# Quarter-sized modulation loads, softmax division before the transposes, and a PSUM tile each for gate and up

## Chip, cores and metric

One core of a Trainium2 chip runs the whole program. The metric is device microseconds of one execution, as the median of the runs shown. TensorE does the matrix products, VectorE, ScalarE and GpSimd the elementwise work, SyncE (SP) issues nearly all transfers. PSUM is the accumulator memory of TensorE's products, in banks of 128 partitions x 512 fp32 numbers; SBUF is the on-chip working memory.

## The reference

Two layers work on 256 latent tokens `x` and 256 context tokens `ctx`, of 1024 numbers each. All data are fp32. Each layer:

```
sh1, sc1, g1, sh2, sc2, g2 = split(silu(c) @ w_mod + b_mod)     # the same for ctx with c_ctx
h   = rms_norm(x) * (1 + sc1) + sh1
a_q, a_k, a_v, conv_u, c_q, c_k, c_v = split(h @ w_in)
mix = [global attention (6 heads), convolution of 31 taps, window attention (6 heads, with a sink)]
x   = x + g1 * (mix @ w_out)
h   = rms_norm(x) * (1 + sc2) + sh2
y   = per token, 2 of 32 experts:  (silu(h @ w_gate[e]) * (h @ w_up[e])) @ w_down[e]
x   = x + g2 * weighted sum of y
```

`w_mod` is 1024 x 6144 a layer, so one modulation vector (shift, scale or gate) needs a 1024 x 1024 block of it, 4 MiB. An expert has three matrices of 1024 x 512, 2 MiB each. Attention's keys are 512 tokens (latent and context); the softmax is exp(score - max) divided by its sum over the keys. The second layer updates only the latent tokens, and the output is their RMS norm.

## The kernel before

**Layer 0's start.** SP issues loads in the order of lines 493 to 499. For j = 0 and 2 it loads four of the eight 128-column chunks of the scale vector (m = 1, in transfers of 512 KB through `load_k4`) and of the shift vector (m = 0, in transfers of 1 MiB), 2 MiB each; for every j the rows 256j to 256j + 255 of `w_in`'s key and value columns (`load_kv`, 512 KB) and of the first convolution columns (`load_u`, 512 KB). `mod_load` (lines 263 to 313) makes a function for each such part. Its `products` multiply `silu(c)` as a 32-column stationary operand in four strips of 32 partitions; its `compute` copies the sums to SBUF on ScalarE (`ms`, line 288), may run other work in between (`between`), picks the rows out and turns them with tiny matmuls (line 295), and adds the bias on VectorE (line 302), with two more VectorE operations for a scale vector (lines 309, 310).

`modulate` (lines 346 to 380) gives three steps for a 128-row chunk k of the hidden state: `h_mul` (VectorE, needs the scale), `h_scale` (ScalarE, needs the shift; writes the rounded high part) and `h_shift` (VectorE, the rest). The products of k want those two parts and the two parts of each weight: `split_w` (lines 382 to 388) for key and value columns on ScalarE and VectorE, `split_u` (523 to 530) for convolution columns on ScalarE and GpSimd. Each product is three matmuls (high by high, high by low, low by high): `product_kv(k)` has twelve, into four PSUM banks `pk`, and `product_u(k)` six, into the tile `pu`. The order of ScalarE, TensorE and VectorE is written out by hand in lines 568 to 609: modulations 0 and 1, dummy matmuls, then eight k, with modulations 2 and 3 around `product_u` of k = 1 and 2. Outside such blocks a planner with a timeline simulation orders the instructions.

**Attention units.** `unit(g, j, i)` (lines 808 to 874) is for a pair of heads and one block of 128 query tokens (i < 2, all 512 keys) or both context blocks (i = 2, 256 keys). It makes scores `S`, takes the max (VectorE, line 825), P = exp on ScalarE with sums collected beside it (line 839), the sums' reciprocal `rl`, transposes P on TensorE (line 853), copies it to `PT` and multiplies by V into `po`. Then `rl` is spread over 64 partitions by a matmul with the identity into the other half of `po` (line 866), copied by ScalarE (`ars`, 870) and multiplied in by VectorE (871), and the result is split into a high part (`mh`, 873) and a low part (874). Layer 0 has 18 units, 12 of one block and 6 of two; layer 1 has 12 of one block. In layer 0 other work, such as the taps of the convolution on VectorE, stands beside them.

**The MoE.** Two experts at a time make a pair, 16 pairs a layer, ordered by hand on TensorE, VectorE and ScalarE (line 1596). `pair` (lines 1344 to 1414) has one stationary tile per expert with up to 64 tokens. It loads twelve tiles of 1 MiB (gate, up and down, two halves for each of two experts) through a ring of 8 slots. Gate (m = 0) goes into half 0 of a two-bank PSUM tile `pgu` and up (m = 1) into half 1, 32 matmuls each; `sil` = silu of half 0 is ScalarE's (line 1358), issued between the two. `act` = up x weight x `sil` is VectorE's (line 1363). Then come four transposes, the down products into the two-bank tile `py`, and `split_y` (lines 1267 to 1276), which reads `py` into YH (ScalarE) and YL (VectorE). `P2` hands out two-bank tiles from a ring of 2, so `pgu` and `py` alternate.

Four lists `at` (lines 1607 to 1622), emptied by `burst(0)` to `burst(3)`, put other work between these steps: the gather of later pairs' tokens, and `adders`, which add the pair before's result to the residual. In most of layer 0's pairs `burst(0)`, which stands between gate and up, has at most VectorE's `onehot`; in layer 1 it has up to three adders, with products of TensorE.

Of the kernel before, what the change touches and what calls it, by code (L numbers as in the profile page):

```python
# [10 lines left out]
F32 = mybir.dt.float32  # L11
# [25 lines left out]
def trunk(ctx: ExitStack, tc: tile.TileContext, t_in, rope, out, cfg):  # L37
# [426 lines left out]
    def layer(l):  # L464
# [27 lines left out]

        first = []
        for j in range(4):
            if l == 0 and j % 2 == 0:
                first += [mod_load(0, 1, 2 * j, 4, load_k4), mod_load(0, 0, 2 * j, 4)]
            load_kv(j)
            if l == 0:
                load_u(j)
# [53 lines left out]
        def mul_to(k):  # L553
            while muls and muls[0] <= k:
                h_mul(muls.pop(0))
# [4 lines left out]
        def product_kv(k, wh, wl, tiles=range(4)):  # L560
            for i in tiles:
                for n, (ww, hh) in enumerate(passes(k, wh, wl)):
                    pe.matmul(pk[i], hh(k, 128 * i, 128), ww, start=k == 0 and n == 0, stop=k == KC - 1 and n == 2)
            if l > 0 and k in cf[0]:
                fill(True)

        order = ExitStack()
        if l == 0:

            order.enter_context(tc.manual_schedule(engines={ET.Activation, ET.PE}))  # L570
            pm = P2("pm")
            pu = P2("pu")
            sk, su = {}, {}

            def modulation(i, work=None):
                first[i](eng=ve, between=work, p=(pm[:, 0, 128 * i:128 * i + 128], pm[:, 1, 16 * i:16 * i + 16]))

            def parts(k):
                h_scale(k)
                h_shift(k)  # L580

            def splits(k):
                sk[k] = split_w(wKV(k), 512, "w", eng=ve)
                su[k] = split_u(k, 0)

            def dummies(n):

                for _ in range(n):
                    pe.matmul(pm[:, 1, 256:512], identb, masks.rearrange("p a b -> p (a b)"), start=True, stop=True)

            modulation(0)
            mul_to(3)
            dummies(4)
            modulation(1)
            dummies(12)
            splits(0)
            parts(0)
            for k in range(KC):
                if k + 1 < KC:
                    splits(k + 1)  # L600
                    parts(k + 1)
                product_kv(k, *sk[k])
                if k in (1, 2):
                    modulation(k + 1, lambda: product_u(pu, k, su[k]))
                    mul_to(k + 3)
                else:
                    product_u(pu, k, su[k])
                    if k > 2:
                        mul_to(k + 3)
        else:  # L610
            for k in range(KC):
                if k + 1 < KC:
                    mul_to(k + 1)
                    h_scale(k + 1)
                h_shift(k)
                product_kv(k, *ws.next())
# [191 lines left out]
        def unit(g, j, i):  # L808
# [37 lines left out]
                ve.tensor_tensor(lsum, lsum, es, op=OP.add)  # L846
            rl = sm.tile([128, 4], F32, name="rl")[:, :n]
            ve.reciprocal(rl, lsum)
            PT = K4("PT", (128, 2, 512))
            for h in range(2):  # L850
                pt = P1("pT")
# [4 lines left out]
            for b in range(nb):  # L856
                for kt in range(4 // nb):
                    for h in range(2):
# [2 lines left out]
                                  V[:, kt if i < 2 else 2 + kt, cv_:cv_ + 64],  # L861
                                  PT[:, h, 128 * (b * 2 + kt):128 * (b * 2 + kt) + 128],
                                  start=kt == 0, stop=kt == 4 // nb - 1)
            for b in range(nb):
                for h in range(2):
                    pe.matmul(po[64 * h:64 * h + 64, 256 + 128 * b:384 + 128 * b],
                              rl[:, h * nb + b:h * nb + b + 1].to_broadcast([128, 64]), ident, start=True, stop=True)
            nq = 128 * nb
            rs = K2("ars", (128, nq), tag="a")
            sc.copy(rs, po[:, 256:256 + nq])  # L870
            ve.tensor_tensor(rs, po[:, 0:nq], rs, op=OP.mult)
            mh = qT[g](2 * j, 128 * i, nq)
            sc.copy(mh, rs)
            ve.tensor_tensor(qT[g](2 * j + 1, 128 * i, nq), rs, mh.bitcast(F32), op=OP.subtract)

        conv(len(taps))
        n = 0
# [466 lines left out]
        def pair(pr, xg, ws, burst, final, finish):  # L1344


            p = P2("pgu")
            for m in range(2):
                for a in range(2):
                    w_ = (load_rows_two([weights_of(pr, m, a, e) for e in range(2)], "we") if final else  # L1350
                          [weight(m, a, e, pr) for e in range(2)])
                    for k in range(4 * a, 4 * a + 4):
                        for e in range(2):
                            pe.matmul(p[64 * e:64 * e + 64, m, :], xg[:, k, 64 * e:64 * e + 64], w_[e](k % 4),  # L1354
                                      start=k == 0, stop=k == KC - 1)
                if m == 0:
                    sil = K2("sil", tag="w")
                    sc.activation(sil, p[:, 0], AF.Silu)  # L1358
                    if final:
                        sqrt_table(sil)  # L1360
                    burst(0)
            act = K2("act", tag="w")
            ve.scalar_tensor_tensor(act, p[:, 1], ws, sil, op0=OP.mult, op1=OP.mult)  # L1363
            burst(1)
            pt = P1("pat")
            for f in range(4):
# [325 lines left out]
```

## Time and profile before

| what | value |
|---|---|
| median of 3 runs (lowest, highest) | 1475.16 us (1473.77, 1477.0) |
| the profiled execution's own time | 1472.71 us |
| span of the profiled execution | 1470.7 us |
| mean granted clock of TensorE | 0.986 of full |
| TensorE busy | 1390.8 us, 95% of the span |
| VectorE busy | 613.4 us, 42% |
| ScalarE busy | 395.7 us, 27% |
| GpSimd busy | 76.7 us, 5% |
| transfers | 481.86 MB, mean 328 GB/s |

The profiled execution's own time is 2.01 us above its span, for what lies around it. Times within the trace are microseconds from the span's start. By the labels of the instructions, the first products of layer 0 run to about 66 us, attention of layer 0 lies between 145 and 235, its MoE between 300 and 815, attention of layer 1 between 873 and 950, and its MoE from 1000 to the end. The busy share is an average over these; TensorE counts as busy while a matmul is in its pipeline, so a share of 100% says that it did not pause, not that it worked at its peak. The DMA share is the mean busy share of the core's 16 DMA engines. In brackets behind an instruction stands how long its engine was idle before it, and what ended this.

### The profile page before, as it was taken

Reading aid. Unit: us, or ns where it says so; the run is one execution under the profiler, and the core shown is the slowest. Engines: PE = TensorE matmul, PEld = TensorE weight load, DVE = VectorE, ACT = ScalarE, POOL = GpSimd, SP = SyncE. Lnnn points to the kernel's source line nnn. Section 1 sums busy time; section 2 is a strip of 40 time slices with the busy share of each in tenths; the row PEclk is TensorE's granted clock in tenths of the full one; section 3 lists DMA queues with packets and bytes.
Section 4 is the critical chain, followed back from the end, with each engine's and each line's share of the span. In section 5 each row is a group of like instructions: output and inputs, shape, how many; then the busy total and the mean of one; then the engine's idle time right before and its main releaser. Section 6 shows DMA issues by size and latency. Waiting matters only on the chain. (4 is left out here: it accounts for less than half of the span.)

```text
span 1470.7 us, 20485 instructions
## 1 busy us (share of the span) xinstructions
PE 1390.8 (95%) x8068; PEld 771.3 (52%) x8068; DVE 613.4 (42%) x1380; ACT 395.7 (27%) x954; POOL 76.7 (5%) x132
## 2 busy tenths in 40 slices
PE   6999999999999999999998998889999999999987
PEld 5776677755445544444434776783433343333332
DVE  4379974443323423233325679853222222222223
ACT  4454675421111111101102565552111011111102
POOL 1202000100000000000001110010000000000000
PEclk9999999999999999999999999999999999999999
DMA  9757204397999999999999590186999999999996
GB/s 350 282 166 284 109 1 172 131 375 306 376 408 414 413 400 406 417 406 414 385 405 389 201 332 31 44 357 280 388 422 421 421 421 421 421 421 419 421 417 255
DMA packets 97412, 481.86 MB, mean 328 GB/s; under 512 B 14068, under 2 KB 22544, under 8 KB 52128
## 3 DMA queue, kind: packets, MB, share of 16 engines
q1 hardware_dynamic: 96576, 478.79, 81.1%
q8 instruction: 66, 1.08, 0.3%
q10 hardware_dynamic: 464, 1.11, 0.2%
q0 software_dynamic: 272, 0.59, 0.1%
q14 instruction: 34, 0.28, 0.0%
HBM read 479.42 MB, written 1.05 MB: 327 GB/s over the span
## 5 line engine op out<-in xcount | busy, mean ns | idle before, releaser
L1354 PE MATMUL pgu<-we,xg 128*64 128x512 f32 x1904 | 449.3, 598 | 30.7 <-DMA we<-in_w_gate_dram 13.6
L1354 PEld LDWEIGHTS pgu<-we,xg 128*64 128x64 f32 x1904 | 142.3, 137 | 324.1 <-issue 246.8
L1408 PE MATMUL py<-we,actT 128*64 128x512 f32 x888 | 202.9, 596 | 0.7 <-ACT actT L1369 0.7
L1363 DVE SCALAR_TENSOR_TENSOR act<-pgu,ws,sil 128x512 f32<-128x512 f32 x32 | 24.0, 751 | 285.1 <-PE pgu L1354 248.6
L1250 DVE SCALAR_TENSOR_TENSOR xT<-pc,mod,xT 128x256 f32<-128x256 f32 x256 | 104.8, 477 | 52.9 <-PE pc L1247 52.2
L1408 PEld LDWEIGHTS py<-we,actT 128*64 128x64 f32 x888 | 63.1, 137 | 117.5 <-issue 113.4
L1304 ACT COPY xg<-pg 128x256 f32<-128x256 f32 x112 | 36.3, 376 | 308.2 <-PE pg L1300 308.2
L1258 DVE TENSOR_TENSOR xo<-xo,pc 128x512 f32<-128x512 f32 x62 | 39.8, 684 | 112.0 <-PE pc L1257 112.0
L1299 PE MATMUL pg<-OH,hH 128*128 128x256 f32 x336 | 83.3, 286 | 0.0
L1300 PE MATMUL pg<-OH,hL 128*128 128x256 f32 x336 | 82.1, 283 | 0.0
L643 DVE SCALAR_TENSOR_TENSOR ca<-gpad,cw,ca 128x512 f32<-128x512 f32 (+1 forms) x120 | 74.2, 619 | 0.9
L1299 PEld LDWEIGHTS pg<-OH,hH 128*128 128x128 f32 x336 | 63.9, 190 | 7.2 <-issue 5.7
L1300 PEld LDWEIGHTS pg<-OH,hL 128*128 128x128 f32 x336 | 64.1, 191 | 0.9
L1358 ACT ACTIVATE sil<-pgu 128x512 f32<-128x512 f32 x32 | 19.1, 598 | 167.6 <-PE pgu L1354 167.6
L281 PE MATMUL pm<-wm,scT 128*32 128x256 f32 (+1 forms) x896 | 60.7, 359 | 3.0 <-DMA wm<-in_w_mod_dram 2.8
L1273 DVE TENSOR_TENSOR Yg<-py,g2r 128x512 f32<-128x512 f32 x31 | 21.3, 688 | 100.7 <-PE py L1408 96.4
L1276 DVE TENSOR_TENSOR YL<-py,YH 128x512 fp32r<-128x512 f32 x32 | 22.1, 690 | 92.7 <-ACT YH L1275 92.7
L1275 ACT CAST YH<-Yg 128x512 fp32r<-128x512 f32 x31 | 19.1, 617 | 141.2 <-DVE Yg L1273 141.2
L1275 ACT CAST YH<-py 128x512 fp32r<-128x512 f32 x32 | 18.7, 585 | 139.0 <-PE py L1408 113.8
L1377 POOL CAST se<-ident 32x128 fp32r<-32x128 f32 x32 | 9.1, 287 | 900.1 <-PE pb L1378 900.1
L1246 PE MATMUL pc<-oht,YH 128*128 128x512 f32 x128 | 53.4, 418 | 1.2 <-ACT YH L1275 1.2
L1247 PE MATMUL pc<-oht,YL 128*128 128x512 f32 x128 | 50.6, 395 | 0.2 <-DVE YL L1276 0.2
(429 smaller groups left out, 2106.0 us busy)
## 6 DMA issues: line engine op xcount, KB each, us to landing
we<-in_w_up_dram SPq DMA_DIRECT2D x112, 1024.0 KB, 9.7
we<-in_w_down_dram SPq DMA_DIRECT2D x111, 1024.0 KB, 12.4
we<-in_w_gate_dram SPq DMA_DIRECT2D x110, 1024.0 KB, 13.5
wm<-in_w_mod_dram SPq DMA_DIRECT2D x44, 1024.0 KB, 9.4
wp<-in_w_gate_dram SPq DMA_DIRECT2D x8, 1024.0 KB, 9.5
wp<-in_w_up_dram SPq DMA_DIRECT2D x8, 1024.0 KB, 9.7
we<-in_w_gate_dram SPq DMA_DIRECT2D x16, 512.0 KB, 12.1
we<-in_w_up_dram SPq DMA_DIRECT2D x16, 512.0 KB, 10.2
```

The lines of the kernel that those rows point to most:

```text
L281: pe.matmul(p[0][32 * q:32 * q + 32], scT[:, kq, :], ws[128 * kq // nr][:, kq % (nr // 128), c:c + n], start=k == 0, stop=k == KC * nq // ...
L643: ve.scalar_tensor_tensor(a, g, wt, a, op0=OP.mult, op1=OP.add)
L1246: pe.matmul(pc, YH[:, 128 * o:128 * o + 128], oht, start=True, stop=False)
L1247: pe.matmul(pc, YL[:, 128 * o:128 * o + 128], oht, start=False, stop=True)
L1250: ve.scalar_tensor_tensor(xT[:, o, sl], pc[:, sl], mod[l][:, 5, o, s:s + 1], xT[:, o, sl], op0=OP.mult, op1=OP.add)
L1258: ve.tensor_tensor(xo[t][:, sl], xo[t][:, sl], pc, op=OP.add)
L1275: sc.copy(YH[:rows, sl], py)
L1299: pe.matmul(dst, hH[t][:, 128 * k:128 * k + 128], rhs, start=t == 0, stop=False)
L1300: pe.matmul(dst, hL[t][:, 128 * k:128 * k + 128], rhs, start=False, stop=t == NT - 1)
L1304: sc.copy(xg[e][:, k - 1:k + 1, :], v[:, :, e])
L1354: pe.matmul(p[64 * e:64 * e + 64, m, :], xg[:, k, 64 * e:64 * e + 64], w_[e](k % 4), start=k == 0, stop=k == KC - 1)
L1408: pe.matmul(py[64 * e:64 * e + 64, h], actT[:, 128 * f + 64 * e:128 * f + 64 * e + 64], wd[e](f % 2)[:, 512 * h:512 * h + 512], start=f == ...
```

## The change

In layer 0's start both vectors load in quarters (two chunks, 1 MiB), one of each before every pair of k's rows, so eight modulations are computed in place of four. Two stand ahead of the products and six inside: for even k around `product_u(k)`, for odd k around `product_kv(k)`. The order by hand is written anew, with 4 and 8 dummies in place of 4 and 12, and the splits and parts of k + 1 move accordingly.

In attention, P is multiplied by the reciprocal sums in place before it is transposed, the first head's on VectorE and the second's on ScalarE. The `rl` products, the `ars` copy and the multiply are gone, and `mh` and the low part come from `po`.

In the MoE, gate and up each take a two-bank tile of `P2` of their own, and use its first bank.

```diff
-            if l == 0 and j % 2 == 0:
-                first += [mod_load(0, 1, 2 * j, 4, load_k4), mod_load(0, 0, 2 * j, 4)]
+            if l == 0:
+                first += [mod_load(0, 1, 2 * j, 2, load_k4), mod_load(0, 0, 2 * j, 2)]
             load_kv(j)
...
             def modulation(i, work=None):
-                first[i](eng=ve, between=work, p=(pm[:, 0, 128 * i:128 * i + 128], pm[:, 1, 16 * i:16 * i + 16]))
+                q = i % 4
+                first[i](eng=ve, between=work, p=(pm[:, 0, 128 * q:128 * q + 128], pm[:, 1, 16 * i:16 * i + 16]))
...
             modulation(0)
-            mul_to(3)
+            mul_to(1)
             dummies(4)
             modulation(1)
-            dummies(12)
+            dummies(8)
+            parts(0)
             splits(0)
-            parts(0)
             for k in range(KC):
-                if k + 1 < KC:
+                if k + 1 < KC and k % 2 == 0:
                     splits(k + 1)
                     parts(k + 1)
-                product_kv(k, *sk[k])
-                if k in (1, 2):
-                    modulation(k + 1, lambda: product_u(pu, k, su[k]))
-                    mul_to(k + 3)
+                if k == KC - 1:
+                    product_kv(k, *sk[k])
+                elif k % 2 == 0:
+                    product_kv(k, *sk[k])
+                    if k + 2 < KC:
+                        modulation(k + 2, lambda: product_u(pu, k, su[k]))
+                        mul_to(k + 3)
+                        splits(k + 2)
+                        continue
                 else:
-                    product_u(pu, k, su[k])
-                    if k > 2:
-                        mul_to(k + 3)
+                    modulation(k + 2, lambda: product_kv(k, *sk[k]))
+                    parts(k + 1)
+                product_u(pu, k, su[k])
...
             ve.reciprocal(rl, lsum)
+            for h in range(2):
+                for b in range(nb):
+                    e = h * nb + b
+                    p = P[:, h, w_ * b:w_ * b + w_]
+                    if h:
+                        sc.activation(p, p, AF.Identity, scale=rl[:, e:e + 1])
+                    else:
+                        ve.tensor_scalar(p, p, rl[:, e:e + 1], None, op0=OP.mult)
             PT = K4("PT", (128, 2, 512))
...
-            for b in range(nb):
-                for h in range(2):
-                    pe.matmul(po[64 * h:64 * h + 64, 256 + 128 * b:384 + 128 * b],
-                              rl[:, h * nb + b:h * nb + b + 1].to_broadcast([128, 64]), ident, start=True, stop=True)
             nq = 128 * nb
-            rs = K2("ars", (128, nq), tag="a")
-            sc.copy(rs, po[:, 256:256 + nq])
-            ve.tensor_tensor(rs, po[:, 0:nq], rs, op=OP.mult)
             mh = qT[g](2 * j, 128 * i, nq)
-            sc.copy(mh, rs)
-            ve.tensor_tensor(qT[g](2 * j + 1, 128 * i, nq), rs, mh.bitcast(F32), op=OP.subtract)
+            sc.copy(mh, po[:, 0:nq])
+            ve.tensor_tensor(qT[g](2 * j + 1, 128 * i, nq), po[:, 0:nq], mh.bitcast(F32), op=OP.subtract)
...
-            p = P2("pgu")
             for m in range(2):
+                p = P2("pgu")[:, 0]
...
-                            pe.matmul(p[64 * e:64 * e + 64, m, :], xg[:, k, 64 * e:64 * e + 64], w_[e](k % 4),
+                            pe.matmul(p[64 * e:64 * e + 64, :], xg[:, k, 64 * e:64 * e + 64], w_[e](k % 4),
...
-                    sc.activation(sil, p[:, 0], AF.Silu)
+                    sc.activation(sil, p, AF.Silu)
...
-            ve.scalar_tensor_tensor(act, p[:, 1], ws, sil, op0=OP.mult, op1=OP.mult)
+            ve.scalar_tensor_tensor(act, p, ws, sil, op0=OP.mult, op1=OP.mult)
```

## Rows read from the trace of the kernel before

**Rows 1.** windows view, MoE stretches: us, busy by engine, clock, DMA share, GB/s
```profile
400.00:680.00 280.00, 271.17 (x1381) 130.81 (x1378) 90.58 (x198) 32.90 (x72) 2.58 (x9) 1.00 1.00 409
1120.00:1340.00 220.00, 207.42 (x933) 84.63 (x931) 49.40 (x86) 27.59 (x62) 2.30 (x8) 1.00 1.01 421
```

**Rows 2.** waits view of TensorE, 400 to 680: waiter, releaser, us, times, longest
```profile
PE pgu L1354 <- ACT sil L1358: 7.3, 9, 1.1
```

**Rows 3.** tile view of sil, whole kernel: who waited (us, times)
```profile
  PE pgu L1354: 10.5, 14
```

**Rows 4.** timeline of ScalarE: first and ninth sil between 404 and 652
```profile
404.38 0.60 ACT L1358 ACTIVATE sil<-pgu 128x512 f32<-128x512 f32 x1 [5.00 <-PE pgu L1354]
...
651.20 0.60 ACT L1358 ACTIVATE sil<-pgu 128x512 f32<-128x512 f32 x1 [5.00 <-PE pgu L1354]
```

**Rows 5.** timeline of TensorE: one pair's gate products and its up products
```profile
644.03 7.04 PE L1354 MATMUL pgu<-we,xg 128*64 128x512 f32 x32
651.85 3.65 PE L1354 MATMUL pgu<-we,xg 128*64 128x512 f32 x16 [0.78 <-ACT sil L1358]
```

**Rows 6.** timeline at a pair's start: first gate product, last reader of py
```profile
330.92 7.04 PE L1354 MATMUL pgu<-we,xg 128*64 128x512 f32 x32
...
333.55 0.68 DVE L1276 TENSOR_TENSOR YL<-py,YH 128x512 fp32r<-128x512 f32 x1
```

**Rows 7.** timeline of layer 0's start, to its first key product
```profile
18.16 1.08 PE L281 MATMUL pm<-wm,scT 128*32 128x128 f32 x32
...
22.02 1.08 PE L281 MATMUL pm<-wm,scT 128*32 128x128 f32 x32 [2.78 <-DMA wm<-in_w_mod_dram]
...
24.86 0.40 ACT L528 CAST wu<-wU 128x256 fp32r<-128x256 f32 x1 [0.74 <-DMA wU<-in_w_in_dram]
...
26.32 0.78 PE L563 MATMUL pkv<-wh,hT 128*128 128x512 f32 x1
```

**Rows 8.** timeline of TensorE: the third modulation, inside the products of k=1
```profile
34.05 0.40 PE L563 MATMUL pkv<-wl,hT 128*128 128x512 f32 x1
...
36.26 0.50 PE L535 MATMUL pu<-hT,wu 128*128 128x512 f32 x1
...
37.75 0.28 PE L295 MATMUL pm<-ident,ms 128*128 128x8 f32 x2
```

**Rows 9.** windows view, two stretches of the start (as rows 1)
```profile
12.00:16.00 4.00, 3.00 (x67) 2.40 (x69) 1.51 (x7) 2.32 (x5) 0.00 (x0) 1.00 1.05 387
20.00:24.00 4.00, 1.47 (x34) 1.13 (x35) 1.18 (x4) 0.77 (x2) 0.00 (x0) 1.00 1.08 365
```

**Rows 10.** windows view, layer 0's units, first and second half (as rows 1)
```profile
150.00:189.00 39.00, 35.47 (x332) 25.95 (x326) 35.08 (x70) 25.01 (x83) 1.49 (x2) 0.96 0.18 72
189.00:217.00 28.00, 28.00 (x281) 21.86 (x280) 22.14 (x62) 20.51 (x71) 0.00 (x0) 1.00 0.01 1
```

**Rows 11.** timeline of TensorE: po and rl products, one-block and two-block unit
```profile
200.87 0.98 PE L860 MATMUL po<-PT,V 128*64 128x128 f32 x13
...
202.10 0.66 PE L853 MATMUL pT<-ident,P 128*128 128x128 f32 x4
...
205.03 0.98 PE L860 MATMUL po<-PT,V 128*64 128x128 f32 x13
...
206.49 0.66 PE L853 MATMUL pT<-ident,P 128*128 128x128 f32 x4
```

**Rows 12.** lines view by form, VectorE: op, shapes, count | busy us, mean ns
```profile
L825 DVE TENSOR_REDUCE mx<-S 128x2 f32<-128x1024 f32 x24 | 29.3, 1221 | 3.1 <-PE S L820 1.9 <-PE S L822 0.8
...
L871 DVE TENSOR_TENSOR ars<-po,ars 128x128 f32<-128x128 f32 x24 | 6.8, 285 | 3.4 <-ACT ars L870 3.4
...
L641 DVE TENSOR_SCALAR ca<-gpad,cw,vb 128x512 f32<-128x512 f32 x2 | 1.1, 542 | 0.0
```

**Rows 13.** lines view by form, ScalarE (columns as rows 12)
```profile
L870 ACT COPY ars<-po 128x128 f32<-128x128 f32 x24 | 6.4, 267 | 23.9 <-PE po L866 23.9
...
L1592 ACT ACTIVATE fs<-xo,finr 128x512 f32<-128x512 f32 x2 | 1.3, 714 | 0.9 <-DVE finr L338 0.9
```

## The prediction

> **What bounds the kernel now.** I read the page's time slices first: two long MoE stretches carry most of the span, so a change at the start or in attention can only move a few microseconds and the pair loop of the MoE needs the closest look. The windows view separates the two loops [rows 1]. In layer 0's, 271.17 us of 280 are TensorE's, and the transfers run at 409 GB/s. In layer 1's, TensorE has idle time, and they run at 421 GB/s, which is the highest steady rate in the page. So layer 1's loop is bound by transfers, and layer 0's by TensorE: in its waits the only large releaser is ScalarE's `sil`, nine times in 280 us, 7.3 us in all, and no transfer [rows 2]. Over the whole kernel it is fourteen times, 10.5 us [rows 3]. The reader is to see that this wait ends on a tile and not on its data: up's products write the other half of the tile that `sil` reads. The first and the ninth `sil` of the stretch begin 246.82 us apart [rows 4], so a pair takes 246.82/8 = 30.85 us. A pair loads twelve tiles of 1 MiB, 12.58 MB, which at 421 GB/s take 29.89 us. That is the floor under any gain there: 0.96 us a pair.
>
> At the start the order is loads, modulation, then products: the first key product starts at 26.32 us, behind a second vector's half that waited for its weights and a cast that waited for `wU` [rows 7]. In layer 0's attention, VectorE is busy for 35.08 us of the first 39, and TensorE for all of the last 28 [rows 10]: two halves with different limits.
>
> **Part 3: a tile each for gate and up.** Gate's products take 7.04 us, and up's begin 651.85 - 644.03 = 7.82 us after gate's first [rows 5]. The last matmul's drain is no part of the pitch: with 0.59 us for one (the rounded mean of the page's costliest group), 15 pitches of (7.04 - 0.59)/15 = 0.43 make 16 x 0.43 = 6.88, and a step without the wait would follow there. So a pair loses 7.82 - 6.88 = 0.94 us, less in those where other work fills part of it. A pair could win 0.94, and the floor allows 0.96. Fourteen pairs: at most 13.2 us; at 0.8, to leave something to a transfer that now comes last, **11.2 us**, which I take, since 10.5 us is what the trace books as waits [rows 3] and restarting the queue behind a wait costs a little more. The low end is half, 14 x 0.4 = 5.6. What is late next is a weight tile, as layer 1 shows. The cost on the other side is the ring: three tiles a pair instead of two, so up of one pair takes the buffer of `py` of the pair before. The last reader of `py` ends at 333.55 + 0.68 = 334.23, and gate's products last from 330.92 to 337.96 [rows 6]: 3.7 us of cover, so I cost this at nothing. If the cover were gone, the wait would be what the readers are late. Layer 1's pairs hide the wait behind the adders already, and gain nothing.
>
> **Part 1: quarters.** Ahead of the first products stand 2 MiB of `x` and `ctx`, a half of each vector (2 MiB each) and k and v's and `u`'s first rows (1 MiB), 7 MiB in all; after, the halves are quarters of 1 MiB, and it is 5 MiB. Before, 5 MiB are in when the first MiB of the second vector's half is: its products start at 18.16 us [rows 7]. Rows of 1 KB load at 365 GB/s instead of 387 [rows 9], for the 2.1 MB of quarters 0.3 us more. With the 26.32 - 24.86 = 1.46 us from the last load's cast to the first product that is 19.9, I say 20.0. The start comes **6.3 us** earlier. In its place, six modulations stand inside the product loop instead of two. One now adds 36.26 - 34.05 less 0.23 (the pitch of the matmul at 34.05), 1.98 us of products, before the covering `pu`, half of its two picks' 0.28, and 0.1 of queue [rows 8]: 2.2, so 4.4 for two. A quarter has half the products: 1.0 + 0.28 + 0.1 = 1.4, six times 8.4: **4.0 us more**. Each pair of them ends in pick, VectorE's add, ScalarE's `h_scale` and VectorE's `h_shift` (some 2.2 us) before the next k's products, with 1.5 us of `product_u` as cover: 0.7, partly filled, I take 0.5 at three places, **1.5 us more**. Queues: SP issues as many bytes in the same order of k; ScalarE's casts for k + 1 stand ahead of the `ms` copy, with some 1 us to spare; POOL gets nothing new. At 365 GB/s the 3 MiB for two k take 8.6 us, under some 11 us of products, so this is hidden. If that cover went, it would be 0.5 us a quarter. Sum: -6.3 + 4.0 + 1.5 = **-0.8**. Bounds: with no stall and a modulation at 1.2 us, -3.3; with a stall of 1.2 at each, +1.5.
>
> **Part 2: P divided.** Removed per unit: the `rl` products on TensorE, the `ars` copy (0.267 us) [rows 13] and the multiply (0.285) [rows 12]. From `po`'s first product to the next transposes is 1.23 us in a one-block unit and 1.46 in a two-block one, whose `rl` passes are twice as many [rows 11]: so 0.23 and 0.46. Layer 0 has 12 and 6 units, 5.5 us; layer 1 has 12, 2.8; together 8.3 at most. Added: half of P on ScalarE, the other on VectorE. No row has these operations on P; the nearest are ScalarE's scaled pass of 512, 0.714 us [rows 13], and VectorE's scaling of 512 out of SBUF, 0.542 [rows 12]. ScalarE is +0.45 a unit, VectorE +0.26. In layer 0's first half nine units stand on VectorE: 9 x 0.26 = +2.3. In the second half TensorE is the bound: gain 2.8. Layer 1 gains up to 2.8, I take 2.5 as it is TensorE's in only part of the time. Off that goes about 2 us where nothing covers a unit (the first and last of each layer): sum, reciprocal and scaling now precede the transposes. Sum +2.3 - 2.8 - 2.5 + 2.0 = **-1.0**. Bounds: all of the 8.3 won, and none of it with +7.5 (30 units by 0.25).
>
> The row of VectorE's scaling runs at one result a cycle, 512 in 0.542 us. The Trainium skill ("VectorE: DVE Perf Modes", Mode 2×_2P) says that such a one-source operation between SBUF tiles makes two a cycle where the outermost dimension is even; by it the scaling would take about 0.3 us, an estimate from that page, and the sum would be some 2 us lower. The nearest row reads a padded tile, and disagrees.
>
> **Sum.** -11.2 - 0.8 - 1.0 = -13.0 us, against the profiled execution's 1472.71 us: 1459.7. The median of the runs is 2.45 us higher, so against it the forecast is **1462 us**. All good ends: -13.2 - 3.3 - 8.3 = -24.8, or 1450. All bad ends: -5.6 + 1.5 + 7.5 = +3.4, or 1479.
>
> **Rivals.** *A, transfers take over in layer 0.* It already moves 409 of 421 GB/s at a DMA share of 1.00 [rows 1], and if a slot comes free late, half of part 3 is paid back: -5.6 - 0.8 - 1.0 = -7.4, or 1468. For it speaks the share of 1.00; against it, that TensorE waits for no transfer there. The Trainium skill ("SBUF — State Buffer", Summary: rules for kernel authors) would plan HBM loads at some 358 GB/s; by this a pair would need 35.1 us, an estimate from that figure, and part 3 would bring nothing; the measured 30.85 us already stands below it.
>
> *B, slower: attention's chain.* In a unit, the scaling waits for sums and reciprocal, and on VectorE it can stand behind the next unit's reduce of 1.221 us. If nothing runs ahead, each one-block unit grows by 1.22 + 0.54 - 0.23 = 1.53 us and each two-block one by 1.22 + 0.54 - 0.46 = 1.30: 24 x 1.53 + 6 x 1.30 = 44.5, less 12.0 of the other parts: +32.5, or 1508. The point from which the kernel is slower: 0.4 us a unit (12.0/30). For it: VectorE is full in the first half [rows 10]. Against: other units' products stand beside it in the planner's order, and TensorE was full in the second half.
>
> *C, part 3 does not do what it says.* The tile's wait goes, and up waits for `py`'s readers, or the order is held by another semaphore: then only -0.8 - 1.0 = -1.8, or 1473. Against it stand the 3.7 us of cover.
>
> **How the numbers follow.** The forecast's chance is 0.66, A's 0.16, B's 0.08, C's 0.10. A measurement of this kernel can tell about 0.2%, 3 us, from no change. Forecast and A are faster by more: 0.82. C is no change: 0.10. B is slower: 0.08. The forecast's own range takes each part's bounds together only in part, 1453 to 1470; up to 1473 it holds A and C, and B, with the far ends, is left out: **1453 to 1473**.
>
> **What the profile would show.** Part 3 right: no wait of up's products for `sil`, a layer-0 pair of 30.0 us (between 29.9 and 30.2), and weight transfers as the new releaser. If it stays over 30.5, A or C holds: A shows transfers as releasers, C shows `py`'s readers or `sil`. Part 1 right: the first key product near 20 us, and layer 0's eighth k ends about where it did, 1 us earlier. Part 2 right: no `rl` products, in the first half of layer 0's attention VectorE fuller than 90%, in the second half fewer TensorE microseconds. A pause of TensorE over 1 us ahead of the transposes, with the scaling as releaser, at most units would be B. A period of the pairs that does not move, or an attention that is longer by over 5 us, would make the forecast wrong.

## The result and the profile after

The changed kernel is slower: 1487.16 us as the median of four runs (1485.45 to 1488.96), against 1474.47 for the kernel before beside it. The ratio is 1.0082, with a 95% interval of 1.0064 to 1.0100. The profiled execution took 1487.36 us, its span is 1485.6 us. The forecast was 1462. Of all the runs below a single one stands far from the others: one of e6's ten took 3460.2 us and counts in e6's median (1476.25 us, 1476.03 without it).

The quickest way to see where the time went is to follow a few landmarks through both traces: starts, in us from the span's start, of the first key product, of the copy of the finished key products (`kn`), of the first scores of layer 0's attention, of layer 0's and layer 1's first `sil`, and of layer 1's first key product and first scores.

| landmark | before | after | later by |
|---|---|---|---|
| first key product | 26.3 | 19.9 | -6.4 |
| products done (`kn`) | 67.6 | 74.8 | +7.2 |
| first scores, layer 0 | 142.3 | 149.5 | +7.2 |
| first `sil`, layer 0 | 313.7 | 334.8 | +21.1 |
| first key product, layer 1 | 811.9 | 822.8 | +10.9 |
| first scores, layer 1 | 872.9 | 883.9 | +10.9 |
| first `sil`, layer 1 | 1001.9 | 1017.3 | +15.4 |
| end of span | 1470.7 | 1485.6 | +14.9 |

So the start loses 7.2 us, layer 0's attention 13.9, its MoE wins 10.2, layer 1's attention loses 4.5, and the rest wins 0.5. One part did what was forecast, and two did not.

**The MoE.** The windows view of after, for the two stretches of [rows 1]:

```profile
400.00:680.00 280.00, 279.97 (x1434) 142.96 (x1434) 95.48 (x213) 34.77 (x77) 2.55 (x9) 1.00 1.00 414
1120.00:1340.00 220.00, 208.13 (x931) 84.63 (x929) 50.24 (x89) 25.92 (x57) 1.98 (x7) 1.00 1.01 421
```

TensorE no longer pauses in the first (279.97 us of 280, 271.17 before). The tile view of `sil`, with its waiters, has no TensorE product of `pgu` left, where [rows 3] had fourteen waits:

```profile
who waited for it (us, times):
  DVE act L1370: 33.5, 3
  PEld pat L1374: 3.3, 6
  PE pat L1374: 1.7, 4
```

The timelines of ScalarE and TensorE answer to [rows 4, 5]. From the first `sil` to the ninth it is 241.53 us, so a pair takes 30.19 us (30.85 before), and gate and up are now one unbroken run of 64 products:

```profile
423.51 0.60 ACT L1365 ACTIVATE sil<-pgu 128x512 f32<-128x512 f32 x1 [5.00 <-PE pgu L1361]
...
665.04 0.60 ACT L1365 ACTIVATE sil<-pgu 128x512 f32<-128x512 f32 x1 [5.00 <-PE pgu L1361]
```

```profile
657.87 13.90 PE L1361 MATMUL pgu<-we,xg 128*64 128x512 f32 x64
```

**The start.** Timelines of TensorE and GpSimd, and below them the windows view of the loop:

```profile
19.91 0.50 PE L563 MATMUL pkv<-wh,hT 128*128 128x512 f32 x1 [0.42 <-ACT wh L385]
...
50.14 0.40 PE L535 MATMUL pu<-hL,wu 128*128 128x512 f32 x1
...
53.30 1.02 PE L535 MATMUL pu<-hT,wu 128*128 128x512 f32 x2 [2.76 <-POOL wu L529]
```

```profile
36.56 0.73 POOL L529 TENSOR_TENSOR wu<-wU,wu 128x256 fp32r<-128x256 f32 x1 [4.79 <-ACT wu L528]
52.29 0.25 POOL L210 TENSOR_SCALAR negsink<-sinkb 128x12 f32<-128x12 f32 x1 [15.00 <-DMA sinkb<-in_sink_dram]
52.53 1.40 POOL L529 TENSOR_TENSOR wu<-wU,wu 128x256 fp32r<-128x256 f32 x2
```

```profile
19.90:50.00 30.10, 28.12 (x261) 21.48 (x262) 12.90 (x31) 10.05 (x25) 3.11 (x4) 1.00 0.94 299
50.00:60.00 10.00, 6.92 (x47) 5.14 (x47) 2.80 (x9) 0.89 (x3) 1.64 (x3) 0.68 0.92 325
60.00:74.80 14.80, 14.13 (x63) 11.06 (x62) 3.48 (x7) 6.23 (x14) 3.64 (x5) 0.99 0.83 300
```

The first key product stands at 19.91 us, where 20.0 was forecast. But GpSimd's queue holds a multiply of the sink values (line 210) among the splits of `w_U`. It waits 15 us for a small load, two splits stand behind it, and TensorE waits 2.76 us for them. The granted clock then falls: 0.68 in the mean of that window, with a part at half (1.2 GHz), after TensorE had stood still.

**Attention.** The lines view by form, for the operations of part 2 (columns as in [rows 12]):

```profile
L874 PE MATMUL po<-PT,V 128*64 128x128 f32 x480 | 43.2, 288 | 8.5 <-DVE PT L868 8.4
...
L860 ACT ACTIVATE P<-P,rl 128x512 f32<-128x512 f32 x24 | 17.5, 729 | 7.3 <-DVE rl L854 7.2
L862 DVE TENSOR_SCALAR P<-P,rl 128x512 f32<-128x512 f32 x24 | 11.6, 483 | 0.4
...
L862 DVE TENSOR_SCALAR P<-P,rl 128x256 f32<-128x256 f32 x12 | 3.7, 350 | 0.2
```

The durations are near those taken (0.729 against 0.714, 0.483 against 0.542 us). What is new are the waits: ScalarE stands 7.2 us for the reciprocal, and TensorE 8.4 us for the copies of the transposed P. The waits view of TensorE from 140 to 260 us shows the same from its side; before, its only such waits there were 3.4, 0.7, 0.4 and 0.3 us. The first three lines are the largest after, the last two the largest before:

```profile
PE po L874 <- DVE PT L868: 6.8, 14, 1.2
PE S L825 <- ACT P L845: 5.9, 7, 2.1
PE pT L867 <- DVE P L862: 0.9, 2, 0.6
...
PE pT L853 <- ACT P L839: 3.4, 2, 2.3
PE S L819 <- ACT P L839: 0.7, 1, 0.7
```

The windows view of the stretch from layer 0's first scores to its first `sil`, before and then after, and last the 28 us of after that answer to the second half of [rows 10]:

```profile
142.26:313.70 171.44, 165.07 (x1275) 124.92 (x1274) 109.22 (x255) 95.18 (x253) 12.12 (x14) 0.98 0.35 133
149.51:334.77 185.26, 166.13 (x1179) 123.35 (x1178) 116.22 (x261) 102.56 (x258) 12.60 (x14) 0.94 0.33 123
...
196.00:224.00 28.00, 24.63 (x205) 17.73 (x205) 20.33 (x51) 19.06 (x60) 0.00 (x0) 1.00 0.10 39
```

TensorE has 96 products fewer in the stretch and is idle for 19.1 us in place of 6.4. Its busy time is 1.1 us longer all the same, at a granted clock of 0.94 against 0.98, so the lower clock probably has a share in the loss, which no run separates. In the later units, where TensorE did not pause before, it works for 24.63 us of 28.

### The profile page after: what moved, and what is told of

The parts are those of the page before. It is cut to its first block, busy times and chain, and to the rows that moved or that the text cites. A ratio compares the mean times of both kernels' runs of the same rounds, so it can differ in the third digit from the quotient of the medians.

```text
span 1485.6 us, 20249 instructions
## 1 busy us (share of the span) xinstructions
PE 1394.8 (94%) x7944; PEld 775.4 (52%) x7944; DVE 622.4 (42%) x1394; ACT 408.0 (27%) x964; POOL 76.9 (5%) x132
## 5 line engine op out<-in xcount | busy, mean ns | idle before, releaser
L1361 PEld LDWEIGHTS pgu<-we,xg 128*64 128x64 f32 x1904 | 147.8, 137 | 308.2 <-issue 240.9
L1365 ACT ACTIVATE sil<-pgu 128x512 f32<-128x512 f32 x32 | 19.1, 598 | 166.3 <-PE pgu L1361 166.3
L1282 ACT CAST YH<-Yg 128x512 fp32r<-128x512 f32 x31 | 19.1, 617 | 140.9 <-DVE Yg L1280 140.9
L874 PE MATMUL po<-PT,V 128*64 128x128 f32 x480 | 43.2, 288 | 8.5 <-DVE PT L868 8.4
## 6 DMA issues: line engine op xcount, KB each, us to landing
we<-in_w_up_dram SPq DMA_DIRECT2D x16, 512.0 KB, 10.2
```

The costliest lines, as they stand in the source:

```text
L874: pe.matmul(po[64 * h:64 * h + 64, 128 * b:128 * b + 128], V[:, kt if i < 2 else 2 + kt, cv_:cv_ + 64], PT[:, h, 128 * (b * 2 + kt):128 * ...
L1282: sc.copy(YH[:rows, sl], py)
L1361: pe.matmul(p[64 * e:64 * e + 64, :], xg[:, k, 64 * e:64 * e + 64], w_[e](k % 4), start=k == 0, stop=k == KC - 1)
```

## The experiments

**Each part alone, and the suspect of the start.** e1, e2 and e3 are the kernel before with one part of the diff. e4 is e1 with line 210 moved behind the product loop:

```diff
-        gp.tensor_scalar(negsink, sinkb.rearrange(...), -1.0, None, op0=OP.mult)
...
         dve_order.close()
+        if l == 0:
+            gp.tensor_scalar(negsink, sinkb.rearrange(...), -1.0, None, op0=OP.mult)
```

> The quarters alone, the rest as before. In the two traces the first key product comes 6.4 us earlier (26.3 to 19.9) and the end of layer 0's products 7.2 us later (67.6 to 74.8). Theory: this part costs about +7 us by itself, so some 1480 (1479 to 1483). Rival: the loss belongs to the three parts together (a planner that orders differently), and quarters alone stay within 3 us of 1474.

> P divided ahead of the transposes, alone. From the first scores to the last multiply by V the traces differ by some 14 us in layer 0 and 5.6 us in layer 1. Theory: this part alone costs +17 to +20 us, so 1491 to 1495. Rival: attention lost its time to the later start and to the work that the planner laid beside it, and this part alone costs under 6 us (below 1481).

> A PSUM tile each for gate and up, alone. In the traces layer 0's MoE is 10.2 us shorter. Theory (as forecast): -10 to -11 us, so 1463 to 1465, no wait of up for sil. Rival: a later transfer gives half back at the turn to layer 1, and it is -5, so 1469.

> The quarters, with GpSimd's multiply of the sink values (which waits for a small load) put behind layer 0's products instead of among the splits. Theory A: the loop lost its time to GpSimd's queue (2.8 us of wait on TensorE, then some 7 us at half clock), and this kernel is 6 us faster than the quarters alone: 1474 (1472 to 1476). Theory B: six modulations with their waits are the cost, GpSimd's wait is only what shows last, and it stays over 1478.

| kernel | median us | before beside it | ratio (95%) |
|---|---|---|---|
| e1 quarters | 1475.36 | 1474.42 | 0.9999 (0.9987 to 1.0012) |
| e2 division | 1492.74 | 1474.42 | 1.0153 (1.0086 to 1.0219) |
| e3 tiles | 1461.61 | 1474.42 | 0.9907 (0.9887 to 0.9927) |
| e4 | 1476.46 | 1474.42 | 1.0010 (0.9999 to 1.0020) |

The ratio is not the quotient of the two medians. The division alone costs 18.3 us by the medians, and the tiles alone bring 12.8, a little more than the 10 to 11 expected. The 18.3 is the least certain number here: e2's four runs took 1490.05, 1490.90, 1494.58 and 1510.00 us, and its interval reaches from 12.7 to 32.3. Without the last run, whose granted clock is 0.935 where the other three have 0.977 to 0.982, it is 16.5, and every difference taken from e2 below changes by these 1.8 us. For the quarters my theory fell: their trace shows the products done at 76.7 us, 9.1 later than before, yet the whole is as long. By the first `sil` of layer 0 it is 6.6 us late (320.3 against 313.7), by layer 1's first key product 5.0. Work behind the loop takes a part up: from the first scores to the first `sil`, e1 takes 168.91 us at a granted clock of 1.00, before it is 171.44 at 0.98, with 1275 products in both. (At the end of the span e1's trace is 3.9 us late where the medians differ by 0.9; executions of one kernel spread by some 5 us.) e4 told nothing, since its edit did not take the multiply away: GpSimd's order is the planner's, and it set the multiply there again. The timeline of GpSimd in e4:

```profile
53.90 0.25 POOL L628 TENSOR_SCALAR negsink<-sinkb 128x12 f32<-128x12 f32 x1 [16.32 <-DMA sinkb<-in_sink_dram]
54.14 1.40 POOL L528 TENSOR_TENSOR wu<-wU,wu 128x256 fp32r<-128x256 f32 x2
```

**The suspect again, and the division taken apart.** e5 gives the multiply to VectorE, whose order there is written by hand. e6 to e8 are e2 with another scaling: by ones, both halves on ScalarE, none.

```diff
             conv_vectors()
+            ve.tensor_scalar(negsink, sinkb.rearrange(...), -1.0, None, op0=OP.mult)
         dve_order.close()
```

The edits of e6 and of e7 (e8 drops the loop that holds these lines):

```diff
-                        sc.activation(p, p, AF.Identity, scale=rl[:, e:e + 1])
+                        sc.activation(p, p, AF.Identity, scale=ones)
-                        ve.tensor_scalar(p, p, rl[:, e:e + 1], None, op0=OP.mult)
+                        ve.tensor_scalar(p, p, ones, None, op0=OP.mult)
```

```diff
-                    if h:
-                        sc.activation(p, p, AF.Identity, scale=rl[:, e:e + 1])
-                    else:
-                        ve.tensor_scalar(p, p, rl[:, e:e + 1], None, op0=OP.mult)
+                    sc.activation(p, p, AF.Identity, scale=rl[:, e:e + 1])
```

> The quarters, with the multiply of the sink values on VectorE behind layer 0's products (GpSimd does the splits alone; in the run before, the planner had set the moved multiply among the splits again). Theory A: without GpSimd's wait of 4 us and the half clock behind it the product loop ends 7 to 9 us earlier (68 to 70 us instead of 76.7), and the whole is 4 to 8 us faster than before: 1467 to 1471. Theory B: what follows takes the earlier end up, as it took up the 9 us of delay of the quarters alone: 1473 to 1476.

> P multiplied by ones in place of the reciprocal sums: the same instructions on VectorE and ScalarE, but the scaling waits for no sum. It leaves the division out. With the division it is 1492.7 us. Theory W (the transposes now wait for exp, both sums, the reciprocal and the scaling in a chain): most of it goes, 1474 to 1482. Theory O (the added 0.48 us of VectorE and 0.72 us of ScalarE a unit are what costs): it stays at 1488 to 1493.

> Both halves of P scaled on ScalarE; VectorE then has less to do in a unit than before the change. Theory O with VectorE as the full engine: 1478 to 1484, some 9.5 us less of VectorE than with the division shared. Theory W: the two scalings stand in one queue, each unit's chain is some 0.5 us longer, and it is 1495 to 1503.

> Neither the scaling of P nor the spreading of the reciprocal sums by TensorE: it leaves the division out. Theories O and W agree: the removed products, copies and multiplies are won, 1465 to 1473. If it stays over 1480, the loss is in neither of them but in the order that the planner made.

Beside 1474.65 for before: e5 1471.62 (0.9974, 0.9964 to 0.9983), e6 1476.25 (1.0014, 1.0004 to 1.0024), e7 1488.36 (1.0088, 1.0072 to 1.0105), e8 1463.10 (0.9923, 0.9905 to 0.9940).

In e5 the products are done at 69.1 us instead of 76.7, and the window from 50 to 60, at 0.68 in the change and 0.64 in e1, has its full clock. So GpSimd's wait and the clock behind it were 7.6 us of the loop; the whole gains some 4 us on e1 of them. The loop came as theory A had it, the whole between the two theories.

```profile
50.00:60.00 10.00, 9.02 (x73) 7.15 (x70) 4.89 (x13) 3.18 (x8) 1.03 (x2) 1.00 0.71 286
```

e6 to e8 split the 18.3 us of the division into three terms. Without `rl` products, copy, multiply and scaling the kernel is 11.6 us faster than before (e8), 1.9 below its expected range. The added scalings, with no sum to wait for, give 13.2 back (e6 less e8). The wait for the sums adds 16.5 (e2 less e6). In the waits view of TensorE from 143 to 262 us, this is e2, and below it e6:

```profile
PE po L868 <- DVE PT L862: 6.6, 14, 1.0
PE S L819 <- ACT P L839: 6.2, 7, 2.2
PE cr L344 <- DVE cn4r L338: 2.5, 1, 2.5
PE pT L861 <- DVE P L856: 1.1, 1, 1.1
```

```profile
PE S L819 <- ACT P L839: 4.8, 3, 2.2
PE po L868 <- DVE PT L862: 1.2, 2, 1.0
```

The windows view from the first scores to the first `sil`, e2 and then e6, shows where TensorE's time went: it is idle for 19.5 us with the sums and for 8.5 with the ones.

```profile
143.37:329.11 185.74, 166.29 (x1179) 123.50 (x1178) 116.07 (x261) 102.77 (x258) 12.95 (x14) 0.95 0.33 123
142.92:315.57 172.65, 164.11 (x1179) 121.73 (x1178) 109.94 (x261) 103.58 (x259) 12.12 (x14) 0.96 0.35 132
```

e7 fell between the theories. Its four runs (1486.03 to 1489.27) lie below all of e2's, but by 0.8 us at the closest, and e2's interval takes e7's in. So the 4.4 us between the medians are not shown to be a gain; what is shown is that a second scaling in ScalarE's queue does not cost the 2 to 10 us that theory W had.

**Company, and a better version.** e9 is parts 1 and 3, e10 parts 1 and 2, e11 is e9 with e5's edit. e12 is e11 with the division behind V's product:

```diff
-                        pe.matmul(po[64 * h:64 * h + 64, 128 * b:128 * b + 128], V[...], PT[...], ...)
+                        pe.matmul(po[:, 128 * b + 64 * h:128 * b + 64 * h + 64], PT[...], V[...], ...)
...
+                    sc.activation(rs[:, c:c + 64], po[:, c:c + 64], AF.Identity, scale=rl[:, h * nb + b:h * nb + b + 1])
+                pe.transpose(pot[:, 128 * b:128 * b + 128], rs[:, 128 * b:128 * b + 128], ident)
```

> Quarters and a tile each, without the division: the change less its second part. The three parts alone measured +0.9, +18.3 and -12.8 us, in sum +6.4; together they measured +12.7. Theory: the parts add, 1462 to 1464, and the 6 us arise where the division meets one of the others. Rival: the 9 us of the late product loop, which the quarters alone get back later in layer 0, are not got back where the MoE is no longer held by ScalarE, and it is 1466 to 1470.

> Quarters and the division, with gate and up in one tile. If they add: +0.9 + 18.3, so 1493 to 1495. If the loss of the late start stays where attention is longer (nothing behind it takes it up): 1498 to 1502.

> A candidate: a tile each for gate and up, the quarters with the sink values' multiply on VectorE, attention as before. Alone they measured -12.8 and -3.0 us: 1458 to 1460 if they add. If the earlier start is lost in the MoE, as fast as the tiles alone: 1461 to 1463.

> The run before, and the division moved: V's product is made with the queries on the partitions, ScalarE divides by the sums as it copies it out of PSUM (two passes of 64 a block), and one transpose a block turns it. No rl products, no ars multiply on VectorE, and nothing is added ahead of P's transposes. Theory W and O: the sums' wait stands off the transposes and VectorE loses 0.285 us a unit, 2 to 8 us faster than the run before. Rival: the two more steps in the chain behind the product (division, transpose) hold the next work up, and it is no faster or up to 5 us slower.

Beside 1473.76: e9 1468.71 (0.9971, 0.9958 to 0.9984), e10 1496.92 (1.0151, 1.0133 to 1.0168), e11 1464.01 (0.9928, 0.9911 to 0.9945), e12 1507.15 (1.0232, 1.0211 to 1.0252). The parts do not add. e10 lies between its two forecasts, 23.2 us over before where the sum is 19.2. e9 is in the range of its rival. With the tiles, the quarters cost 7.8 us (-5.0 against -12.8) that they do not cost alone. Some of it can be placed: in layer 1, from the first scores to the first high part of the convolution (`cH`), e1 takes 82.89 us and e9 86.22, with the same code. Here are both ends, e1 and then e9:

```profile
877.92 0.47 PE L825 MATMUL S<-kH,qT 128*128 128x512 f32 x1
...
960.81 0.70 ACT L806 CAST cH<-cy 128x256 fp32r<-128x256 f32 x2
```

```profile
870.70 0.48 PE L825 MATMUL S<-kH,qT 128*128 128x512 f32 x1
...
956.92 0.70 ACT L806 CAST cH<-cy 128x256 fp32r<-128x256 f32 x2
```

The windows view of the two stretches, e1 and then e9:

```profile
877.92:960.81 82.89, 74.45 (x627) 58.33 (x627) 71.10 (x183) 50.23 (x135) 5.66 (x8) 0.96 0.23 84
870.70:956.92 86.22, 77.00 (x627) 59.37 (x627) 72.06 (x183) 50.13 (x135) 5.81 (x8) 0.92 0.21 78
```

The same 627 products keep TensorE busy for 2.55 us longer, at a granted clock of 0.92 against 0.96, so most of the 3.3 us goes with the clock. What made it fall is not shown. VectorE has its instructions in another order in e9, presumably because the planner simulates time and meets a shorter MoE ahead; that this order is the cause is argued, not shown. e11 is no faster than e3 (the intervals overlap), so no version that keeps the division is shown to beat the tiles alone, 0.9907 of before. e12 is a clear miss, 43 us slower than e11 where its rival allowed 5, and its waits view of TensorE from 143 to 290 us begins with a stop for the division, where the rival had it:

```profile
PE pot L878 <- ACT ars L875: 12.0, 17, 2.1
PE po L867 <- DVE PT L860: 4.5, 13, 0.4
```

**What the wait holds up, and the last combinations.** e13 is e2 with the scalings written into tiles `Q` that nobody reads. e14 is parts 2 and 3, e15 the whole change with e5's edit.

```diff
-                        sc.activation(p, p, AF.Identity, scale=rl[:, e:e + 1])
+                        sc.activation(q, p, AF.Identity, scale=rl[:, e:e + 1])
-                        ve.tensor_scalar(p, p, rl[:, e:e + 1], None, op0=OP.mult)
+                        ve.tensor_scalar(q, p, rl[:, e:e + 1], None, op0=OP.mult)
```

> The scalings wait for the sums as in the division, on the same engines, but write a tile that nobody reads, and the transposes take P as exp left it; it leaves the division out. The division measured 1492.7, the scaling by ones 1476.3, no scaling 1463.1. Theory T (TensorE's transposes in the chain are the cost): 1474 to 1479, as with the ones. Theory Q (the queues of VectorE and ScalarE that hold a waiting scaling are): 1487 to 1493.

> Division and tiles, the start as before. If they add: +18.3 - 12.8, so 1479 to 1481; then the quarters cost some 7 us in the company of the others, where alone they cost nothing. If it is 1485 or more, the division loses in the company of the tiles.

> The whole change with the sink values' multiply on VectorE, so without GpSimd's wait in the product loop. Theory: the late start of 5 to 7 us is what the change keeps of the quarters, and this is 4 to 7 us faster than the change: 1480 to 1483. Rival: as with the tiles, the order that the planner makes in layer 1 takes it, 1485 to 1488.

Beside 1475.08: e13 1482.85 (1.0053, 1.0033 to 1.0073), e14 1484.01 (1.0059, 1.0039 to 1.0080), e15 1481.66 (1.0040, 1.0025 to 1.0055). e13 lies between the theories: 6.6 us above the ones, 9.9 below the division. The windows view of 28 us of the later units, e2, e6 and e13, and last e13's whole stretch from the first scores to the first `sil`:

```profile
190.00:218.00 28.00, 24.62 (x200) 17.52 (x202) 20.09 (x52) 19.80 (x62) 0.00 (x0) 1.00 0.19 78
190.00:218.00 28.00, 28.00 (x234) 20.11 (x235) 21.73 (x66) 24.19 (x74) 0.00 (x0) 1.00 0.15 62
190.00:218.00 28.00, 28.00 (x251) 21.33 (x251) 23.34 (x63) 25.52 (x78) 0.00 (x0) 1.00 0.01 3
...
141.93:322.07 180.14, 163.81 (x1179) 121.98 (x1178) 113.99 (x270) 104.79 (x265) 13.29 (x14) 0.92 0.33 126
```

In the later units TensorE pauses only where the transposes stand behind the sums; with the scalings aside it is as full as with the ones. So the 9.9 us come when the transposes wait. The 6.6 us are not the queues' share alone. In e13 TensorE does wait for other work of VectorE (3.0 us for a `PT` copy, 2.3 for `tq`, from 142 to 262 us), as theory Q has it; but e13 also frees the transposes of the scaling itself, in which e6 has them wait, and its granted clock in the stretch is 0.92, in e6 0.96. The planner orders each of these kernels anew, so these terms hold its choices too. e15 is 5.5 us faster than the change, so GpSimd's wait is in the change's time, and not taken up there as it was in e1. e14 is 8.9 us over before, where 5.5 would be the sum of its parts, and lies between its two forecasts; 2.3 of these 3.4 us are again in layer 1's attention, which takes 90.2 us in e14 and 87.9 in e2. From e14 to the whole change it is 3.8 us more.

## Why the prediction was wrong

**Part 3 was right.** 11.2 us were forecast and 12.8 measured alone; the pair takes 30.19 us, at the edge of the 29.9 to 30.2 named. `py`'s readers never hold up `up`, so rival C is out, and so is rival A, with no transfer among TensorE's waits from 400 to 680 us. The weight transfers named as the new releaser do not show there either: the waits view has no wait of TensorE left, and the transfers rose to 414 GB/s, short of layer 1's 421. In e3's trace 10.8 of the 12.4 us won are layer 0's MoE; the rest lies outside the part's mechanism.

**Part 2 is the step that failed.** The term was -1.0 us, with +7.5 as the worst bound; alone it measured +18.3. The working counted instructions on VectorE and ScalarE, and costed the new chain (both exps, both sums, the reciprocal, the scaling, then the first transpose) only "where nothing covers a unit (the first and last of each layer)", at 2 us. It stands in every unit. By the prediction's own terms the work without the wait was -3.0 us (+2.3 - 2.8 - 2.5) and came out at +1.6 (e6); the new chain was +2.0 and came out at 16.5 (e2 less e6, 14.7 without e2's last run). Before, the first half's transposes could begin when that half's exp was done, and the reciprocal had until the `rl` products, which come last. After, both halves wait for both sums. In the first unit the transposes start 0.83 us behind the start of the first exp before (145.49 us) and 3.00 behind it after (152.74). The timelines of TensorE, before and after:

```profile
146.32 1.33 PE L853 MATMUL pT<-ident,P 128*128 128x128 f32 x8 [1.06 <-ACT P L839]
...
155.74 1.81 PE L867 MATMUL pT<-ident,P 128*128 128x128 f32 x8 [0.28 <-DVE P L862]
```

The sum of the forecast also took TensorE's 100% in the second half [rows 10] as a reason why only removed TensorE work counts there; in e6 and e13 it is as full in the later units, and with the transposes behind the sums (e2) it works for 24.62 us of 28: it was full because its order had no such wait in it. Rival B had the place, with a chance of 0.08, and too high a price: 44.5 us for a unit with no overlap at all, where 18.3 came. Its sign, a pause of over 1 us ahead of the transposes at most units with the scaling as releaser, did not come: layer 0's attention has two waits of the transposes for the scaling, the longer of 0.6 us, and most of TensorE's waiting shows at V's products, for the copies of the transposed P, and at the scores, for exp. Its mechanism was the scaling behind the next unit's reduce; in the timelines of the later units the scaling stands ahead of that reduce, and it is the chain of sums that is late. The other side was missed as well: removing the `rl` work is worth 11.6 us, more than the 8.3 called its most; that bound counted TensorE's share alone, and the copy and the multiply that go with it presumably make the difference.

**Part 1** was forecast at -0.8 and measured 0.0 (ratio 0.9999; +0.9 by the medians) alone, but by errors that cancel. The start was right to 0.1 us. The loop was to grow by 5.5 us. In the change it grew by 13.6, from 41.3 to 54.9, and in e1 by 15.7, to 56.9. Without GpSimd's wait and the clock behind it, it is 48.9 us in e5 and in e15, so these two make 6.0 us in the change and 8.0 in e1. The prediction said "POOL gets nothing new", which is true of its work and not of its queue: the multiply waited for the same load before, and the splits behind it were not yet wanted. An earlier start wants them earlier. GpSimd's timeline before:

```profile
50.44 0.26 POOL L210 TENSOR_SCALAR negsink<-sinkb 128x12 f32<-128x12 f32 x1 [8.28 <-DMA sinkb<-in_sink_dram]
```

The rest, 7.6 against 5.5, comes with the modulations. The windows view of the loop, before and in e15, has 4.7 us more of busy TensorE where 4.0 were taken for the modulations, and 2.9 us more of idle TensorE where 1.5 were taken for the stalls:

```profile
26.30:67.60 41.30, 41.25 (x286) 32.26 (x285) 16.41 (x35) 16.02 (x36) 7.58 (x11) 0.98 0.89 328
19.99:68.89 48.90, 45.94 (x367) 35.52 (x368) 19.31 (x46) 17.15 (x40) 8.20 (x11) 1.00 0.95 319
```

That later stages take part of the delay up was not in the working.

**The sum.** Alone the parts make +0.9 + 18.3 - 12.8 = +6.4, and the change +12.7. Of the 6.3 us between, 3.4 are there as soon as the division and the tiles are together (e14), and 2.9 come with the quarters, which cost 3.8 in that company and 0.9 alone. Some 2 to 3 us of such differences stand in layer 1's attention in the traces; the rest stays open. Each figure that takes e2 in holds its doubt of 1.8 us.

One reading of a row was wrong too. VectorE's scaling of 512 numbers took 0.542 us, which I took for one result a cycle against the rule of the Trainium skill ("VectorE: DVE Perf Modes", Mode 2×_2P). The new operation comes in two sizes, 350 and 483 ns for 256 and 512: 0.52 ns for each further number, and 0.217 us that stay. At that page's clock of 0.96 GHz this is two results a cycle, so the trace agrees with the rule; my estimate of 0.3 us left out the fixed part. The row's own operation says the same: before, it took 410 ns for 256 numbers and 542 for 512. Two slips in the sums moved nothing: the mean of the costliest group is 0.598 us and not 0.59, and part 1's bounds are -3.5 and +1.3 by their own terms.

## What to carry to other kernels

Before moving an operation ahead of a step, write down what that step waited for and what it waits for afterwards, in every iteration: a new dependence costs where it breaks the overlap, and busy shares do not show it. When work starts earlier, look in each in-order queue for an instruction whose own release does not move, and what is queued behind it. And where a planner orders the rest, the parts of a change must be measured together as well as alone.

## What the runs showed of the hardware

TensorE writes one PSUM bank while ScalarE reads another without a pause: with a tile each, up's products run on behind gate's (64 in 13.90 us) while `sil` reads gate's bank, and 14 waits are gone. So the wait before was one of the program's tile and not of the banks, as far as two banks of different tiles show it; two banks of one tile without the wait were not tried.

V's product is cheaper with 64 stationary columns for each head than its count suggests. In the change, a unit's 16 passes of 128 numbers take 1.09 us together. In e12, with all 128 columns stationary and half as many numbers to move, eight take 1.10 us, and a unit has two such groups. The first row is from the timeline of after, the second from e12's:

```profile
925.87 1.09 PE L874 MATMUL po<-PT,V 128*64 128x128 f32 x16
```

```profile
207.42 1.10 PE L867 MATMUL po<-V,PT 128*128 128x64 f32 x8 [0.24 <-DVE PT L860]
```
